# Loading the merge's numerators through GpSimd's queue and issuing its stores one step later, in a hybrid attention layer

## The chip, the cores and the metric

The kernel runs on 1 core of one Trainium2 chip. The metric is device time in microseconds (us) of the whole program; lower is better. A core has five engines that each take their instructions in order: TensorE (PE in the profile), VectorE (DVE), ScalarE (ACT), GpSimd (POOL) and SyncE (SP). A transfer (DMA) is issued by one of them, from its own place in that engine's order: an issue that has to wait holds up whatever stands behind it on the same engine. All queues share the core's 16 DMA engines.

## What is computed

One inference step of a decoder layer: 1,024 prompt rows and 64 sample rows (together 1,088) of width 2,048.

```
h = x @ w_in + b_in               # split into q, k, v, z_a | 3 x (q_g, k_g, v_g), z_b | g_a, g_b
o_a = sliding-window attention with sinks (16 heads)
o_b = sum_g softmax_g(lse_g) * dilated attention g    # g = 0..2, 8 heads each
y_a = o_a * silu(z_a);  y_b = o_b * silu(z_b)
m = sigmoid(g_a) * (y_a @ w_br_a) + sigmoid(g_b) * (y_b @ w_br_b)
x = LayerNorm(alpha * x + m @ w_out)
```

It also returns the new key and value windows.

## The kernel before

All products run on TensorE in three passes: every float32 operand is split into a high and a low part, and hi\*hi, lo\*hi and hi\*lo are added up in PSUM (lines 170 to 172). The input projection has 78 column tiles of 128. The first 34 (q, k, v) come first; while the other 44 (z, g_a, g_b) are multiplied, attention, decoding and last the **merge** are worked off beside them. Then follow the two output products, in three parts.

The order is written out by hand. `in_proj` calls `tick` once per 12 matmuls (4 rows of k by 3 products), here called a *step*; a column tile has 12 steps. `Beside.tick` first runs what was put off with `after(n, f)` for n steps, and then lets the background generator advance at a set rate, 0.9 of its own steps per step during the merge. Every engine therefore has one fixed order in which the projection's work and the merge's work alternate:

- **ACT**: casts a weight part to its high half (L89), evacuates a column tile from PSUM with the bias (L954), computes the merge's sigmoids (L865) and issues the merge's stores (L890).
- **DVE**: makes the low half of a weight part (L90), and does the merge's multiplications and additions (L854, L858, L859, L866, L867).
- **SP**: issues the weight loads (L78, 512 KB), the stores of the evacuated tiles (L956, 192 or 160 KB) and, before the change, the merge's loads of numerators (L841).
- **POOL**: issues the merge's loads of w (L844) and of z (L847).

Weight parts are split two parts ahead of the matmuls that use them (`Weights.ahead`, 4 buffers). A tile z of the projection has 2 buffers, so an evacuation L954 waits until the store L956 of the tile but one before has landed.

The merge goes over 12 rows of heads, i = 0..11. For i < 8 (mixer A) there is one *item*, (i, 0); for i = 8..11 (mixer B) there are three, (i, 0), (i, 1) and (i, 2). `load(i, g)` brings the numerator num(i, g) (544 KB for g = 0, 512 KB otherwise), the weights w(i, g) as two broadcasts of 256 KB each, and with g = 0 also z(i), 544 KB. `add(i, 0)` multiplies num by w (L854); `add(i, 1)` and `add(i, 2)` multiply (L858) and add to the numerator of g = 0 (L859). `gate(i, half)` computes o \* z \* sigmoid(z) in place of z (L865, L866, L867), and y(i), 544 KB, is stored from there.

Buffers decide what a load waits for: num with g > 0 has one buffer, so num(i, 2) waits for L858 of (i, 1), and num(i+1, 1) for L858 of (i, 2). w has two, so w(i, 2) needs the buffer that add(i, 0) has finished with. num with g = 0 has two, and waits for the gates of i-2. z has two, and z(i+2) waits until the store y(i) has landed.

Loads are called one item ahead (`steps`): at item n the next item's `load` stands before `add(n)`, but the load of (i, 2) stands after `add(i, 1)`.

Of the kernel before, what the change touches and what calls it, by code (L numbers as in the profile page):

```python
# [105 lines left out]
def layer_kernel(ctx: ExitStack, tc: tile.TileContext, A, O, S):  # L106
    nc = tc.nc
# [24 lines left out]
    def after(n, f):  # L132

        later.append((now[0] + n, f))
# [75 lines left out]
    with tc.tile_pool(name="qp", bufs=2, side="right") as qp:  # L210
# [152 lines left out]
        for g in range(4):  # L363
            w = (128,) + WINS
            n = w[g] - NQ
# [465 lines left out]
    def merge():  # L831
        with tc.tile_pool(name="mp", bufs=1, side="right", reuse_waits="tile") as mp:
            wb = weights_b(mp)
            items = [(i, g) for i in range(12) for g in range(1 if i < 8 else 3)]
            got, zs = {}, {}

            def load(i, g):
                num = mp.tile([P, T], F32, tag="num" if g else "o", name="num", bufs=1 if g else 2)
                w = mp.tile([P, NT], F32, tag="w", name="w", bufs=2)
                n = NT if g else T  # L840
                nc.sync.dma_start(out=num[:, :n], in_=S["num"][i + 4 * g, :, :n])  # L841
                src = S["wa"][2 * i:2 * i + 2] if i < 8 else S["wb"][g, 2 * (i - 8):2 * (i - 7)]
                for h in range(2):
                    nc.gpsimd.dma_start(out=w[HD * h:HD * (h + 1)], in_=src[h].partition_broadcast(HD))  # L844
                if g == 0:
                    zs[i] = mp.tile([P, T], F32, tag="z", name="z", bufs=2)
                    nc.gpsimd.dma_start(out=zs[i], in_=S["z"][i])  # L847
                got[i, g] = num, w

            def add(i, g):  # L850
                num, w = got[i, g]
                o = got[i, 0][0]
                if g == 0:
                    nc.vector.tensor_mul(o[:, :NT], o[:, :NT], w)  # L854
                    return
                nv = num[:, :NT].rearrange("p (c j) -> p j c", c=DILS[g])
                wv = w.rearrange("p (j c) -> p j c", c=DILS[g])
                nc.vector.tensor_mul(wv, nv, wv)  # L858
                nc.vector.tensor_add(o[:, :NT], o[:, :NT], w)  # L859

            def gate(i, half):
                c = slice(T // 2 * half, T // 2 * (half + 1))
                o, z = got[i, 0][0], zs[i]
                sg = mp.tile([P, T // 2], F32, tag="sg", name="sg")
                nc.scalar.activation(sg, z[:, c], AF.Sigmoid)  # L865
                nc.vector.tensor_mul(z[:, c], z[:, c], sg)  # L866
                nc.vector.tensor_mul(z[:, c], z[:, c], o[:, c])  # L867

            def steps():
                load(0, 0)  # L870
                for _ in range(3):
                    yield
                for n, (i, g) in enumerate(items):
                    nxt = items[n + 1] if n + 1 < len(items) else (0, 2)
                    if nxt == (8, 0):
                        for _ in wb:
                            pass
                    if nxt[1] < 2:
                        load(*nxt)
                    yield  # L880
                    add(i, g)
                    if g == 1:
                        load(*nxt)
                    yield
                    if nxt[0] != i:
                        gate(i, 0)
                        yield
                        gate(i, 1)
                        yield
                        nc.scalar.dma_start(out=S["y"][i], in_=zs[i])  # L890

            for _ in steps():
                next(wb, None)
                yield
# [107 lines left out]
    for part, (a, b) in enumerate(CHUNKS):  # L1002
        last = part == len(CHUNKS) - 1
        n = b - a
# [111 lines left out]
        if not last:  # L1116
            after(2, lambda: nc.scalar.activation(m4[:, :, 2], m4[:, :, 1], AF.Sqrt, bias=epst))
            nxt = load_g(0, *CHUNKS[part + 1])
            for i, (t, c) in enumerate(tiles):
                h, v = hs[i], mv[:, 4 * i:4 * i + 4]  # L1120
                after(3, lambda v=v: norm_start(v))
                for u in range(0, DM, 512):
                    n = 4 + 14 * i + 3 * (u // 512)
# [3 lines left out]
                        out=O["y"][t:t + P, u:u + 512], in_=h[:, u:u + 512]))  # L1127
# [130 lines left out]
```

## Time and profile before

| | us |
|---|---|
| median of 3 runs | 2760.76 (2759.12 to 2764.41) |
| the profiled execution, its own time | 2763.79 |
| its span | 2761.8 |
| PE busy | 2727.9 (99%) |
| DVE busy | 1477.8 (54%) |
| ACT busy | 928.5 (34%) |
| POOL busy | 855.2 (31%) |

The page's slices show PE at nine tenths or more in all but the first and the last, with a granted clock of 0.995 on average. The merge lies between 1883 and 2055 us of the span. In this stretch the DMA engines move 45.56 MB, 265 GB/s on average, where the whole span has 169 GB/s. The profile gives the time from issue to landing only for DMAs that POOL issues; for those of SP and ACT it is seen where somebody waits for the landing.

### The profile page before, as it was taken

What the parts mean: (1) busy time and instruction counts of PE and PEld (TensorE: products, weight loads), DVE (VectorE), ACT (ScalarE), POOL (GpSimd) and SP (SyncE); (2) the same over time, 40 slices, a digit from 0 to 9 for tenths busy, and PEclk for the clock granted to TensorE, in tenths of its full rate; (3) what the DMA queues carried; (4) which work ended last, traced back from release to release, by engine and by line L of the source; (5) the groups of instructions that cost most, each with busy time, mean ns of one, the idle gap of its engine ahead of it and who ended that gap; (6) DMA issues with size and microseconds to landing.
All of it is one profiled execution on the core that took longest, in us unless ns stands there. A gap on an engine that the chain in (4) does not pass through costs nothing.

```text
span 2761.8 us, 43516 instructions
## 1 busy us (share of the span) xinstructions
PE 2727.9 (99%) x16643; PEld 2625.8 (95%) x16643; DVE 1477.8 (54%) x2648; ACT 928.5 (34%) x1857; POOL 855.2 (31%) x905
## 2 busy tenths in 40 slices
PE   8999999999999999999999999999999999999997
PEld 8999999999999999999999998889999989988986
DVE  5444442443436777777665432124555556855866
ACT  4122222222223444444433332223224434433442
POOL 1112122131126666677677723433110000000001
PEclk9999999999999999999999999999999999999999
DMA  7345454464464333454445534657876745754763
GB/s 227 102 129 178 161 183 156 142 203 153 161 222 126 113 113 109 129 151 145 145 146 147 149 102 155 198 186 220 277 243 232 245 129 172 235 187 137 244 221 99
DMA packets 206088, 467.64 MB, mean 169 GB/s; under 512 B 28936, under 2 KB 128648, under 8 KB 203128
## 3 DMA queue, kind: packets, MB, share of 16 engines
q1 hardware_dynamic: 167512, 312.33, 35.8%
q0 software_dynamic: 36272, 145.19, 16.7%
q10 hardware_dynamic: 2096, 7.34, 0.7%
q8 instruction: 131, 2.15, 0.3%
q14 instruction: 77, 0.63, 0.1%
HBM read 365.17 MB, written 144.21 MB: 184 GB/s over the span
## 4 chain that ended last, share of the span: by engine, by line
PE 90%; DMA 4%; DVE 4%; ACT 1%; issue 1%; SPq 0%; POOL 0%; ACTq 0%; DVEq 0%; POOLq 0%
PE psd L170 21%; PE psd L172 21%; PE psd L171 21%; PE psd L1064 3%; PE psd L1063 3%; PE psd L1062 3%; PE psa L425 2%; PE psd L1021 2%; PE psd L1020 2%; PE psd L1019 2%; PE psa L487 1%; PE psa L486 1%; PE psa L1064 1%; PE psa L1063 1%; PE psa L1062 1%; PE psa L1021 1%
## 5 line engine op out<-in xcount | busy, mean ns | idle before, releaser
L170 PE MATMUL psd<-xhi,whi 128*128 128x384 f32 (+1 forms) x3712 | 1224.3, 330 | 16.8 <-ACT whi L89 12.3
L172 PE MATMUL psd<-xhi,wlo 128*128 128x384 f32 (+1 forms) x3712 | 1217.5, 328 | 0.5 <-DVE wlo L90 0.4
L171 PE MATMUL psd<-xlo,whi 128*128 128x384 f32 (+1 forms) x3712 | 1216.7, 328 | 0.1
L170 PEld LDWEIGHTS psd<-xhi,whi 128*128 128x128 f32 x3712 | 699.1, 188 | 32.9 <-issue 14.0
L90 DVE TENSOR_TENSOR wlo<-wraw,whi 128x512 fp32r<-128x512 f32 x648 | 449.0, 713 | 478.4 <-ACT whi L89 473.9
L172 PEld LDWEIGHTS psd<-xhi,wlo 128*128 128x128 f32 x3712 | 698.6, 188 | 2.0 <-DVE wlo L90 2.0
L171 PEld LDWEIGHTS psd<-xlo,whi 128*128 128x128 f32 x3712 | 699.1, 188 | 0.4 <-DVE xlo L226 0.4
L89 ACT CAST whi<-wraw 128x512 fp32r<-128x512 f32 x648 | 386.7, 618 | 393.2 <-PE psa L1063 151.7
L460 POOL PARTITION_ALL_REDUCE md<-s x160 | 310.1, 1938 | 67.2 <-ACT s L457 44.0
L446 POOL PARTITION_ALL_REDUCE md<-s x160 | 214.4, 1340 | 177.5 <-DVE s L435 65.0
L1126 POOL DMA_DIRECT2D o_y<-h x24 | 13.0, 542 | 573.0 <-DVE h L994 562.4
L477 DVE TENSOR_TENSOR pl<-s,ph 128x512 fp32r<-128x512 f32 (+1 forms) x160 | 128.0, 800 | 100.3 <-ACT ph L476 98.3
L1062 PE MATMUL psd<-whi,m 128*128 128x512 f32 x384 | 149.8, 390 | 0.5 <-ACT whi L89 0.5
L1063 PE MATMUL psd<-whi,m 128*128 128x512 f32 x384 | 149.8, 390 | 0.0
L1064 PE MATMUL psd<-wlo,m 128*128 128x512 f32 x384 | 149.7, 390 | 0.0
L457 ACT ACTIVATE s<-s 128x256 f32<-128x256 f32 (+1 forms) x160 | 75.9, 475 | 196.2 <-DVE s L456 196.0
L954 ACT ACTIVATE z<-psd,bias 128x384 f32<-128x384 f32 x132 | 73.8, 562 | 191.9 <-PE psd L172 126.2
L312 POOL DMA_DIRECT2D s_sq<-raw x20 | 11.5, 576 | 371.9 <-DVE raw L295 371.9
L1021 PE MATMUL psd<-y,wlo 128*128 128x384 f32 (+1 forms) x384 | 125.7, 327 | 0.1
L1019 PE MATMUL psd<-y,whi 128*128 128x384 f32 (+1 forms) x384 | 125.4, 326 | 0.0
L1020 PE MATMUL psd<-y,whi 128*128 128x384 f32 (+1 forms) x384 | 125.4, 326 | 0.0
L284 ACT ACTIVATE raw<-psd,bias 128x384 f32<-128x384 f32 (+1 forms) x79 | 44.2, 559 | 199.4 <-PE psd L172 199.4
(209 smaller groups left out, 3314.4 us busy)
## 6 DMA issues: line engine op xcount, KB each, us to landing
wraw<-w_in SPq DMA_DIRECT2D x152, 512.0 KB
wraw<-w_out SPq DMA_DIRECT2D x96, 512.0 KB
wraw<-w_br SPq DMA_DIRECT2D x72, 512.0 KB
o_c<-c POOLq DMA_DIRECT2D x64, 510.0 KB, 8.5
qst<-s_qs SPq DMA_DIRECT2D x80, 256.0 KB
s_zg<-z SPq DMA_DIRECT2D x64, 192.0 KB
kv<-ktb POOLq DMA_DIRECT2D x48, 256.0 KB, 3.7
kv<-vb POOLq DMA_DIRECT2D x48, 256.0 KB, 3.2
```

The source lines that it names most:

```text
L89: self.nc.scalar.copy(hi, raw)
L90: self.nc.vector.tensor_tensor(out=lo, in0=raw, in1=hi.bitcast(F32), op=ALU.subtract)
L170: nc.tensor.matmul(o, lhsT=h, rhs=xhi[k][:, a:b], start=(k == 0), stop=False)
L171: nc.tensor.matmul(o, lhsT=h, rhs=xlo[k][:, a:b], start=False, stop=False)
L172: nc.tensor.matmul(o, lhsT=l, rhs=xhi[k][:, a:b], start=False, stop=(k == KT - 1))
L446: nc.gpsimd.partition_all_reduce(u["md"][:, 0], top, P, RED.max)
L460: nc.gpsimd.partition_all_reduce(u["md"][:, 1], s[:, 1 if n == 1 else 2], P, RED.add)
L1019: nc.tensor.matmul(o, lhsT=h, rhs=yt[k][:, 0, :n], start=st, stop=False)
L1021: nc.tensor.matmul(o, lhsT=l, rhs=yt[k][:, 0, :n], start=False, stop=en)
L1062: nc.tensor.matmul(pt, lhsT=h, rhs=whi, start=st, stop=False)
L1063: nc.tensor.matmul(pt, lhsT=l, rhs=whi, start=False, stop=False)
L1064: nc.tensor.matmul(pt, lhsT=h, rhs=wlo, start=False, stop=en)
```

## The change

Two lines of `merge` are changed. The loads of numerators are issued by GpSimd instead of SyncE, at the head of each `load`; and the store of y(i) is put off by one step, so that it stands behind the next step's work in ACT's order.

```
@@ -838,7 +838,7 @@
                 n = NT if g else T
-                nc.sync.dma_start(out=num[:, :n], in_=S["num"][i + 4 * g, :, :n])
+                nc.gpsimd.dma_start(out=num[:, :n], in_=S["num"][i + 4 * g, :, :n])
@@ -887,7 +887,7 @@
                         gate(i, 1)
                         yield
-                        nc.scalar.dma_start(out=S["y"][i], in_=zs[i])
+                        after(1, lambda z=zs[i], i=i: nc.scalar.dma_start(out=S["y"][i], in_=z))
```

On POOL, at the end of the merge, where the rows i = 9 to 11 of mixer B are loaded, stood before:

```order
L844 DMA w<-s_wb 64x1024 x6
L847 DMA z<-s_z 128x1088
L844 DMA w<-s_wb 64x1024 x6
L847 DMA z<-s_z 128x1088
L844 DMA w<-s_wb 64x1024 x4
```

and now, from z(10) on:

```order
L847 DMA z<-s_z 128x1088
L841 DMA num<-s_num 128x1024
L844 DMA w<-s_wb 64x1024 x2
L841 DMA num<-s_num 128x1024
L844 DMA w<-s_wb 64x1024 x2
L841 DMA num<-s_num 128x1088
L844 DMA w<-s_wb 64x1024 x2
L847 DMA z<-s_z 128x1088
```

Every pair of loads of w now stands behind the load of its numerator, and so behind what that load waits for.

On SP, in the same part of the merge, a piece of the difference:

```order
-L841 DMA num<-s_num 128x1024
-L841 DMA num<-s_num 128x1088
-L78 DMA wraw<-w_in 128x1024
-L841 DMA num<-s_num 128x1024
-L78 DMA wraw<-w_in 128x1024
-L956 DMA s_zg<-z 128x384 x2
-L841 DMA num<-s_num 128x1024
+L78 DMA wraw<-w_in 128x1024 x2
+L956 DMA s_zg<-z 128x384 x2
+L956 DMA s_zg<-z 128x320
```

All 20 loads of numerators are gone from SP; the weight loads and the stores of evacuated tiles stand alone there.

On ACT, at one of the places where its order changes (a store of y, L890):

```order
 L865 ACTIVATE sg<-z 128x544
 L954 ACTIVATE z<-psd,bias 128x320
+L89 CAST whi<-wraw 128x512
 L890 DMA s_y<-z 128x1088
-L89 CAST whi<-wraw 128x512
```

The cast that stood behind the store now stands ahead of it. On PE and DVE nothing moves.

## Rows read from the trace of the kernel before

**Rows 1.** Waits of PE from 1883 to 2055 us: total, times, longest
```profile
PE psd L170 <- ACT whi L89: 5.2, 1, 5.2
PE psd L170 <- ACT z L954: 4.4, 2, 2.5
```

**Rows 2.** Windows of 20 us: length, busy per engine (instructions), PE's granted clock, DMA share, GB/s
```profile
1920.00:1940.00 20.00, 17.45 (x106) 17.13 (x105) 14.73 (x20) 6.20 (x10) 3.69 (x8) 1.00 0.79 259
...
1960.00:1980.00 20.00, 20.00 (x122) 20.00 (x121) 7.16 (x9) 5.87 (x10) 4.18 (x8) 1.00 0.91 299
1980.00:2000.00 20.00, 14.79 (x78) 13.98 (x77) 13.20 (x13) 2.21 (x4) 3.61 (x7) 0.83 0.81 242
```

**Rows 3.** ACT in order of time: start, length, what [idle before, what ended it]
```profile
1928.53 1.28 ACT L865 ACT_TABLE_LOAD   x1 [8.66 <-DMA z<-s_z]
...
1993.92 0.53 ACT L954 ACTIVATE z<-psd,bias 128x320 f32<-128x320 f32 x1 [15.51 <-DMA s_zg<-z]
```

**Rows 4.** SP in order of time; a row spans its issues and the waits between them
```profile
1964.35 18.73 SPq L841 DMA_DIRECT2D num<-s_num  x3
...
1983.65 11.14 SPq L956 DMA_DIRECT2D s_zg<-z  x3
...
2013.69 0.39 SPq L841 DMA_DIRECT2D num<-s_num  x1
```

**Rows 5.** DVE in order of time: L858 of the items with g > 0, and two low halves
```profile
1980.05 2.03 DVE L858 TENSOR_TENSOR w<-num,w 128x1024 f32<-128x1024 f32 x1 [6.51 <-DMA w<-s_wb]
...
1986.14 2.01 DVE L858 TENSOR_TENSOR w<-num,w 128x1024 f32<-128x1024 f32 x1 [2.20 <-DMA num<-s_num]
...
1994.98 0.69 DVE L90 TENSOR_TENSOR wlo<-wraw,whi 128x512 fp32r<-128x512 f32 x1 [4.18 <-ACT whi L89]
...
1999.05 2.03 DVE L858 TENSOR_TENSOR w<-num,w 128x1024 f32<-128x1024 f32 x1 [0.24 <-DMA num<-s_num]
...
2007.17 2.02 DVE L858 TENSOR_TENSOR w<-num,w 128x1024 f32<-128x1024 f32 x1 [3.31 <-DMA num<-s_num]
...
2021.98 2.03 DVE L858 TENSOR_TENSOR w<-num,w 128x1024 f32<-128x1024 f32 x1 [2.87 <-DMA num<-s_num]
...
2027.81 2.03 DVE L858 TENSOR_TENSOR w<-num,w 128x1024 f32<-128x1024 f32 x1 [1.93 <-DMA num<-s_num]
...
2040.09 2.03 DVE L858 TENSOR_TENSOR w<-num,w 128x1024 f32<-128x1024 f32 x1 [3.80 <-DMA w<-s_wb]
...
2046.19 2.02 DVE L858 TENSOR_TENSOR w<-num,w 128x1024 f32<-128x1024 f32 x1 [1.54 <-DMA num<-s_num]
...
2052.23 0.68 DVE L90 TENSOR_TENSOR wlo<-wraw,whi 128x512 fp32r<-128x512 f32 x1
```

**Rows 6.** PE in order of time, at the merge's end
```profile
2052.97 0.44 PE L172 MATMUL psd<-xhi,wlo 128*128 128x384 f32 x1
```

**Rows 7.** POOL in order of time: one load of z, three pairs of loads of w
```profile
1919.50 0.56 POOL L847 DMA_DIRECT2D z<-s_z  x1 [9.51 <-DMA s_y<-z]
...
1971.92 1.02 POOL L844 DMA_DIRECT2D w<-s_wb  x2 [1.34 <-DVE num L854]
...
1989.70 1.03 POOL L844 DMA_DIRECT2D w<-s_wb  x2 [4.51 <-DVE num L859]
...
2010.75 1.03 POOL L844 DMA_DIRECT2D w<-s_wb  x2 [6.55 <-DVE num L859]
```

**Rows 8.** Time to landing, line 844 (w, 256 KB) and then line 847 (z, 544 KB)
```profile
DMA to landing us min/median/max: 3.6/7.2/9.9
...
DMA to landing us min/median/max: 4.0/8.4/11.3
```

**Rows 9.** The chain that ended last: start, length, what
```profile
1994.88 4.05 DMA num<-s_num
```

**Rows 10.** A window of 2 us: length, PE busy (instructions), granted clock, DMA share, GB/s
```profile
1980.00:1982.00 2.00, 2.00 (x14) 1.00 0.02 8
```

**Rows 11.** Waits of ACT from 1883 to 2055 us: total, times, longest
```profile
ACT whi L89 <- DVE z L867: 10.3, 5, 2.5
```

More of the change, by code (lines that the diff above doesn't have):

```diff
@@ L840, in load @@
                 n = NT if g else T
-                nc.sync.dma_start(out=num[:, :n], in_=S["num"][i + 4 * g, :, :n])
+                nc.gpsimd.dma_start(out=num[:, :n], in_=S["num"][i + 4 * g, :, :n])
                 src = S["wa"][2 * i:2 * i + 2] if i < 8 else S["wb"][g, 2 * (i - 8):2 * (i - 7)]
@@ L889, in steps @@
                         yield
-                        nc.scalar.dma_start(out=S["y"][i], in_=zs[i])
+                        after(1, lambda z=zs[i], i=i: nc.scalar.dma_start(out=S["y"][i], in_=z))
             for _ in steps():
```

## The prediction

> **What bounds the kernel now.** I looked first at what PE waits for, stretch by stretch. In the merge's stretch it waits three times, 5.2 us for a cast and twice, 4.4 us in all, for an evacuation [rows 1]; the change touches no other stage, so I set no term elsewhere. Counting matmuls gives the same loss with the clock in it: an undisturbed 20 us hold 122, so one takes 0.164 us, while 1920 to 1940 us hold 106 and 1980 to 2000 us only 78 [rows 2]. That is 16 x 0.164 = 2.6 us and 44 x 0.164 = 7.2 us; the second has 5.2 us of standing and 2.0 us of the clock, which after PE had stood was granted at 0.83 on average, part of the window at 1.2 instead of 2.4 GHz. The third wait is 4.4 - 2.5 = 1.9 us. Together **11.7 us, 0.42% of the time, is all that the change can win**.
>
> Then I asked what stood behind these waits. For the first, ACT sat 8.66 us until z(3) had landed [rows 3], and z(3) had been issued only after 9.51 us of waiting for the store y(1) to land [rows 7]: a loop of store, landing, load, landing over two items. For the second, ACT sat 15.51 us until an earlier tile's store had landed [rows 3]. SP issued that store at 1983.65, because its three loads of numerators from 1964.35 on filled 18.73 us [rows 4]: num(8, 2) had to wait for L858 of (8, 1), which ran from 1980.05 to 1982.08 [rows 5]. While SP stood there the DMA engines were nearly empty, share 0.02 from 1980 to 1982 us [rows 10].
>
> At the merge's end another limit shows. The last low half that DVE makes inside the merge ends at 2052.23 + 0.68 = 2052.91 [rows 5], and PE's first product with it starts at 2052.97 [rows 6]. DVE is just in time: no reserve is left. What DVE's chain of merge items gains or loses up to there, PE gains or loses one for one, within the 11.7 us. So I add up that chain.
>
> **The change part by part.**
>
> *SP loses 20 issues.* Short in themselves, and PE never waits for SP's issuing. What counts is where they waited. Num(9, 1) could have gone at 1986.14 + 2.01 = 1988.15 [rows 5] and went at 1994.88 [rows 9], 6.7 us late, behind a tile's store that itself waited for ACT. Num(10, 1) could have gone at 2009.19 [rows 5] and went at 2013.69 [rows 4], 4.5 us late. Both held L858. Without them w is the next to come late: w(9, 1), second half issued at 1990.2 [rows 7], lands by the median of 7.2 us [rows 8] at 1997.4, and L858 began at 1999.05 [rows 5]: 1.65 us won. For w(10, 1) it is 2011.26 + 7.2 = 2018.5 against 2021.98: 3.5 us. At (11, 1) the wait was for w already [rows 5], nothing won. **Sum -5.2 us**, bounds 0 (w still later) and -11.2 (w beside num).
>
> *DMA time that lay idle is filled.* The weight load and the two stores behind num(8, 2), 512 + 2 x 192 KB, start before 1980 us instead of after 1983. At 299 GB/s [rows 2] they are 3.1 us of traffic taken out of the crowd after it. I take the 2.0 us of rows 10: **-2.0 us**, bounds 0 and -3.1.
>
> *POOL gains 20 issues of half a microsecond* [rows 7], as much as one issue of w; POOL is busy 3 to 4 of 20 us [rows 2], so that is covered by its waiting. Were that cover gone, 20 x 0.51 = 10 us would stand on the path. The cost is in the order. Before, w(8, 2) was issued at 1971.92 [rows 7], 8 us ahead of L858 of (8, 1). Now it stands behind num(8, 2), which waits for that L858, and so in each of the four rows of mixer B. The numerator alone took 4.05 us from issue to use [rows 9]; now the next L858 needs the numerator and 512 KB behind it. Added: 0.2 us for the slower issue (0.51 against some 0.3) and 512 KB at 299 GB/s, 1.75 us, so 1.95 us each. **4 x 1.95 = +7.8 us.** No row shows this directly. From below, w's data hide in the numerator's and only the 1.0 us of issuing and the 0.2 remain: +4.8. From above, w takes its median 7.2 us [rows 8] from its second issue, 1.0 us after the numerator's: 8.2 - 4.05 = 4.15 each, +16.6. I take 1.95, nearer to the lower end, since w then follows a queue that has just run empty and the shortest landing is 3.6 us [rows 8].
>
> *The order between z and num.* Num(i+1, 0) now stands behind z(i), which waits for a store to land. It is needed only after the gates of i, by which time z(i) has landed and been used, so this costs nothing; if it landed late, add(i+1, 0) would wait, about 2 us each time. But z(i) no longer has that numerator ahead of it in the DMA engines, 544 KB or 1.86 us at 299 GB/s.
>
> *The store one step later.* One step is 12 x 0.164 = 1.97 us. ACT's casts no longer wait for DVE's gate: 10.3 us in five waits [rows 11], which I count as nothing by themselves, since ACT is busy 6 of 20 us [rows 2] and PE met only the three waits above. The loop of y and z gets longer by up to 1.97 us; on the other hand y(i+1) too now falls behind z(i+2), another 1.86 us off z. Each loop: -2 x 1.86 + 1.97 = -1.75 us. Three such loops in a row lead up to L858 of (8, 1); I count two, since the merge's own pace, 0.9 of its steps per step, takes the rest. **-3.5 us**, bounds 0 and -5.3.
>
> Sum: -5.2 - 2.0 + 7.8 - 3.5 = **-2.9 us**. The profiled execution took 2763.79 us, 2.0 more than its span, and would take 2760.9; it lies 3.0 us above the median, so for the median 2760.76 - 2.9 = **2757.9 us**. A measurement of this kernel can tell about 0.2%, 5.5 us, from no change, so this is a forecast of no visible change, on the fast side.
>
> **The rivals.**
>
> *Most of the loss comes back.* The second PE wait came from SP's blocking alone: DVE too sat 4.18 us for that cast [rows 5]. If w costs only the lower bound (+4.8) and the loops and the idle time give their upper ones (-5.3, -3.1, with -5.2 as above), the chain is 8.8 us shorter: 2752.0 us. For it speaks that the traffic needs less than the time: 299 GB/s were reached where 242 were moved in the worst window [rows 2]. Against it, that DVE has no reserve at the end [rows 6].
>
> *Slower: the loss of the early w.* The four distances from L858 of (i, 1) to that of (i, 2) are 6.1, 8.1, 5.8 and 6.1 us [rows 5], mean 6.5. If w lands at its median behind the numerator, each grows by 4.15 us, and if nothing of the idle DMA time is won, 16.6 - 8.7 = +7.9 us: 2768.7 us. The point from which the change loses is 10.7/4 = 2.7 us more per pair, a distance of 9.2 us; it is visible from some 4 us more, 10.5 us. For it speaks that w's landing was 7.2 us in the median [rows 8]; against it, that much of that was queueing behind loads which now go elsewhere.
>
> *GpSimd's transfers start later than SyncE's.* Loads of 256 KB from POOL landed at best after 3.6 us [rows 8]; the 512 KB from SP took 4.05 [rows 9], and 3.2 without 256 KB at 299 GB/s: up to 0.4 us later per load. Two per row of mixer B stand on the chain, 8 x 0.4 = 3.4 us with the fraction kept, and the time is 2761.3. Against it stands a 544 KB load of POOL that landed after 4.0 us [rows 8]. The Trainium skill, "DMA: Bandwidth & Descriptors", Specifications, gives a first byte after about 1 us on GpSimd's path and 0.6 us on SyncE's, and its section "Issuing engine by pattern" puts simple loads on SyncE: by that rule the move is wrong, and an estimate from that page's figures is 8 x 0.4 = 3.2 us. On this rule the trace does not decide: its two rows point to either side.
>
> **How the numbers follow.** My forecast gets 0.38, the later start 0.10, the recovery 0.34, the loss of the early w 0.18. The first two are within 0.2%: 0.48; faster 0.34, slower 0.18. The forecast's own range, with the later start in it, is the band within 0.2%, 2755.3 to 2766.3. The range for 8 in 10 goes down to 2750.5, near the 2749.1 at which PE waits for nothing in the merge, and up to 2767.0, short of the slow rival's full price.
>
> **What would show it.** In the changed profile SP's stores should follow their evacuations at once, and the wait of 15.51 us for such a store should be gone. L858 of (8, 1) should begin earlier than 1980.05; the distances within a pair should grow from 6.5 to some 8.5 us, and those from (i, 2) to (i+1, 1) shrink from 12.9, 14.8 and 12.3. PE should lose 8 to 9 us instead of 11.7, most of it late in the merge and for DVE's low halves or casts behind L858. I am wrong if distances within a pair stay at 6.5 us (then faster), if they pass 10.5 us (then slower), or if PE waits outside the merge change.

## The result, and the profile after

The changed kernel is **slower**: 2779.56 us in the median (2773.18 to 2784.8, 4 runs) beside 2761.36 (4 runs) of the kernel before, a ratio of 1.0065 with an interval of 1.005 to 1.0079. The loss is 18.2 us, and the time lies outside the forecast's range. The profiled execution took 2784.8 us, the longest of the four, and is 21.0 us longer than the profiled one of before (2763.79), so what the traces show of the loss is somewhat more than the medians do.

PE's waits come first, as before, now with the waits of the two engines that this change concerns. Waits of the kernel after, from 1883 to 2100 us: engine and line waiting, what it waited for, total, times, longest.

```profile
POOL num L841 <- DVE w L858: 61.4, 7, 13.4
...
DVE w L858 <- DMA w<-s_wb: 43.1, 7, 8.7
...
ACT z L954 <- DMA s_zg<-z: 25.0, 6, 5.7
...
PE psd L170 <- ACT z L954: 10.0, 3, 6.2
...
PE psd L172 <- DVE wlo L90: 8.8, 3, 4.7
...
PE psd L170 <- ACT whi L89: 3.0, 1, 3.0
```

PE stands for 10.0 + 8.8 + 3.0 = 21.8 us where it stood for 9.6 [rows 1], and 8.8 of them are for DVE's low halves, for which it had not waited at all. The store that held ACT for 15.51 us [rows 3] holds it for 5.7 at most now: that wait is gone, and the time did not come with it. Two lines have come to the top. POOL waits 61.4 us in seven places to issue a numerator, because the numerator's one buffer is free only once L858 has run; and DVE's L858 in turn waits 43.1 us in seven places for w, where it had waited for w 10.3 us in two.

Windows of the kernel after, columns as in [rows 2]; the last three are short ones inside the others.

```profile
1920.00:1940.00 20.00, 17.77 (x97) 17.46 (x96) 17.73 (x26) 9.99 (x15) 5.29 (x10) 0.91 0.92 254
1940.00:1960.00 20.00, 18.44 (x113) 18.12 (x112) 9.07 (x13) 4.44 (x9) 4.76 (x9) 1.00 0.99 313
1980.00:2000.00 20.00, 13.10 (x71) 12.46 (x69) 8.02 (x7) 2.16 (x4) 5.07 (x10) 0.87 0.66 183
2000.00:2020.00 20.00, 15.88 (x82) 15.56 (x82) 10.39 (x11) 1.99 (x4) 4.24 (x9) 0.84 0.80 228
2020.00:2040.00 20.00, 17.00 (x86) 17.00 (x87) 10.76 (x12) 4.22 (x8) 4.96 (x10) 0.77 0.89 277
2060.00:2080.00 20.00, 15.99 (x86) 15.41 (x85) 9.21 (x11) 5.02 (x9) 0.00 (x0) 0.91 0.30 94
1981.00:1987.00 6.00, 4.61 (x29) 4.29 (x27) 2.15 (x2) 1.05 (x3) 0.00 (x0) 1.00 0.17 59
1998.00:2006.00 8.00, 5.09 (x18) 5.09 (x19) 6.01 (x8) 2.46 (x4) 1.49 (x3) 0.57 1.02 263
2009.00:2011.00 2.00, 2.00 (x13) 2.00 (x12) 1.97 (x2) 0.00 (x0) 0.19 (x1) 1.00 0.05 18
```

Against 122 matmuls in an undisturbed 20 us, the six windows lack 25 + 9 + 51 + 40 + 36 + 36 = 197, by 0.164 us each 32.3 us. Before it was 11.7. The difference, 20.6 us, is the 21.0 us by which the profiled executions differ: nearly the whole loss lies in the merge, most of it after 1980 us, in mixer B. Some of it is the clock's: after PE stood, 0.77 to 0.91 were granted on average where full windows have 1.00. And the DMA engines still run empty in between, at a share of 0.17 from 1981 to 1987 us and of 0.05 from 2009 to 2011.

DVE of the kernel after in order of time, the rows that answer to [rows 5], L858 of the items with g > 0:

```profile
1984.82 1.95 DVE L858 TENSOR_TENSOR w<-num,w 128x1024 f32<-128x1024 f32 x1 [8.34 <-DMA w<-s_wb]
...
1995.69 1.91 DVE L858 TENSOR_TENSOR w<-num,w 128x1024 f32<-128x1024 f32 x1 [7.06 <-DMA w<-s_wb]
...
2008.48 2.03 DVE L858 TENSOR_TENSOR w<-num,w 128x1024 f32<-128x1024 f32 x1 [3.94 <-DMA w<-s_wb]
...
2017.48 1.89 DVE L858 TENSOR_TENSOR w<-num,w 128x1024 f32<-128x1024 f32 x1 [5.11 <-DMA w<-s_wb]
...
2028.54 2.02 DVE L858 TENSOR_TENSOR w<-num,w 128x1024 f32<-128x1024 f32 x1
...
2038.84 2.02 DVE L858 TENSOR_TENSOR w<-num,w 128x1024 f32<-128x1024 f32 x1 [6.42 <-DMA w<-s_wb]
...
2050.81 2.03 DVE L858 TENSOR_TENSOR w<-num,w 128x1024 f32<-128x1024 f32 x1 [3.49 <-DMA w<-s_wb]
...
2063.39 2.02 DVE L858 TENSOR_TENSOR w<-num,w 128x1024 f32<-128x1024 f32 x1 [8.69 <-DMA w<-s_wb]
```

The distances from (i, 1) to (i, 2) are 10.9, 9.0, 10.3 and 12.6 us, mean 10.7, where they were 6.5. Those from (i, 2) to (i+1, 1), called *gaps* below, are 12.8, 11.1 and 12.0 where they were 12.9, 14.8 and 12.3. L858 of (8, 1) comes 4.8 us later than before, and all waits that end here now end with w.

Why w is late is seen on POOL, kernel after, in order of time:

```profile
1987.06 0.56 POOL L841 DMA_DIRECT2D num<-s_num  x1 [13.37 <-DVE w L858]
1987.61 1.05 POOL L844 DMA_DIRECT2D w<-s_wb  x2
1988.62 0.56 POOL L841 DMA_DIRECT2D num<-s_num  x1
1989.17 1.05 POOL L844 DMA_DIRECT2D w<-s_wb  x2
1990.18 0.57 POOL L847 DMA_DIRECT2D z<-s_z  x1
1997.90 0.54 POOL L841 DMA_DIRECT2D num<-s_num  x1 [7.14 <-DVE w L858]
...
2053.14 0.56 POOL L841 DMA_DIRECT2D num<-s_num  x1 [9.66 <-DVE w L858]
```

POOL stands 13.37 us for L858 of (8, 1). Behind it stand not only w(8, 2) but num(9, 0), w(9, 0) and z(9), and within 3.7 us they all go out: 2.6 MB with num(8, 2), on one queue. They land in the order of issue: num(8, 2) at 1991.3, the second half of w(8, 2) at 1995.5, num(9, 0) at 1999.5, z(9) at 2004.9. The next numerator, num(9, 1), is issued at 1997.90 behind the rest of them. The chain that ended last shows how long these transfers took. Kernel after: start, length, what.

```profile
1972.12 10.81 DMA num<-s_num
...
1987.06 4.25 DMA num<-s_num
...
1997.90 8.60 DMA num<-s_num
...
2010.81 4.11 DMA num<-s_num
...
2019.67 4.65 DMA num<-s_num
...
2030.85 4.03 DMA num<-s_num
...
2041.16 8.04 DMA num<-s_num
...
2054.19 9.08 DMA w<-s_wb
```

There are two kinds. Num(8, 2), num(9, 2) and num(10, 2) (1987.06, 2010.81, 2030.85), issued when the loads ahead of them on POOL's queue had landed, take 4.0 to 4.3 us. Num(9, 1) and num(11, 1) (1997.90, 2041.16), issued behind the burst, take 8.6 and 8.0, where num(9, 1) took 4.05 on SP's queue [rows 9]; num(10, 1) between them got through in 4.65. These last three came in right behind what was still ahead of them: 1.6, 1.7 and 1.3 us after z(9), z(10) and z(11), which took 14.7, 8.7 and 13.9 us. From issue to landing, z(9) to z(11), kernel after:

```profile
DMA to landing us min/median/max: 8.7/13.9/14.7
```

Num(8, 1), issued right behind z(8), takes 10.81. One row does not fit: num(11, 2), issued at 2053.14 with all loads ahead of it landed and only its own w behind it, took 9.1 us, and why stays open.

### The profile page after: what moved, and what is told of

Read it like the earlier page. It is cut to its first block, busy times and chain, and to the rows that moved or that the text cites. A ratio compares the mean times of both kernels' runs of the same rounds, so it can differ in the third digit from the quotient of the medians.

```text
span 2783.0 us, 43507 instructions
## 1 busy us (share of the span) xinstructions
PE 2731.8 (98%) x16643; PEld 2628.0 (94%) x16643; DVE 1476.7 (53%) x2648; ACT 928.2 (33%) x1857; POOL 866.2 (31%) x925
## 4 chain that ended last, share of the span: by engine, by line
PE 87%; DMA 6%; DVE 3%; issue 2%; ACT 1%; POOL 0%; SPq 0%; ACTq 0%; POOLq 0%; DVEq 0%
PE psd L170 20%; PE psd L172 20%; PE psd L171 20%; PE psd L1062 3%; PE psd L1064 3%; PE psd L1063 3%; PE psa L425 2%; PE psd L1020 2%; PE psd L1019 2%; PE psd L1021 2%; DMA num<-s_num 2%; PE psa L487 1%; PE psa L486 1%; PE psa L1062 1%; PE psa L1064 1%
## 5 line engine op out<-in xcount | busy, mean ns | idle before, releaser
L312 POOL DMA_DIRECT2D s_sq<-raw x20 | 11.5, 576 | 372.2 <-DVE raw L295 372.2
```

## The experiments

Five theories were put to the test. **1**: w comes late because it stands behind its own numerator. **2**: the later store delays y and z. **3**: a numerator that goes through GpSimd's queue is slower in itself. **4**: the numerator's wait for its one buffer, harmless in SP's order, is what costs once it stands in POOL's. **5**: too much is on one queue, so the transfer that is needed next comes in behind others that are not. Each of the kernels e1 to e12 was timed in five rounds, 5 to 12 executions. The table has the median of the kernel and of the kernel before on the same chip, the recorded ratio with its interval, and from the one profiled execution the distances within pairs and the gaps, worked out from the starts of L858. The ratio is not the quotient of the two medians, which differs by up to 0.1% (by the medians e3 would be 1.0050, e4 and e6 1.0009, e5 1.0042); losses of 0.1 or 0.2% are therefore uncertain.

| kernel | median us | before | ratio, interval | within pairs | gaps |
|---|---|---|---|---|---|
| before | | | | 6.1 8.1 5.8 6.1 | 12.9 14.8 12.3 |
| after | 2779.56 | 2761.36 | 1.0065, 1.005 to 1.0079 | 10.9 9.0 10.3 12.6 | 12.8 11.1 12.0 |
| e1 loads alone | 2776.20 | 2762.25 | 1.0056, 1.0043 to 1.0068 | 9.2 9.0 9.9 11.3 | 10.8 12.0 10.2 |
| e2 store alone | 2761.44 | 2762.25 | 0.9997, 0.9989 to 1.0006 | 5.8 8.5 5.7 6.8 | 14.2 13.1 13.4 |
| e3 w first | 2776.14 | 2762.25 | 1.0043, 1.0027 to 1.0058 | 6.1 6.1 6.9 7.7 | 16.5 13.3 16.7 |
| e4 only g = 0 moved | 2764.21 | 2761.69 | 1.0014, 1.0005 to 1.0023 | 6.3 7.4 7.9 6.1 | 12.5 11.4 12.4 |
| e5 only g > 0 moved | 2773.27 | 2761.69 | 1.005, 1.0038 to 1.0063 | 11.8 11.9 11.5 12.1 | 8.7 10.8 9.0 |
| e6 changed, two buffers | 2764.29 | 2761.69 | 1.0017, 1.0008 to 1.0026 | 3.7 7.4 3.8 4.0 | 11.7 12.7 15.9 |
| e7 before, two buffers | 2760.74 | 2761.69 | 1.0003, 0.9993 to 1.0012 | 3.8 4.7 3.8 3.9 | 13.6 13.8 15.2 |
| e8 short queue | 2767.61 | 2761.71 | 1.0019, 1.0008 to 1.003 | 6.3 7.5 6.7 8.7 | 9.9 13.8 11.3 |
| e9 only g > 0, two buffers | 2761.86 | 2761.71 | 1.0, 0.999 to 1.001 | 3.7 8.9 3.8 3.8 | 11.7 12.7 15.4 |
| e10 rate 0.8 | 2753.58 | 2761.71 | 0.9965, 0.9951 to 0.9978 | 6.9 5.9 6.7 6.5 | 12.4 14.7 16.7 |
| e11 rate 0.8, two buffers | 2750.43 | 2761.71 | 0.9957, 0.9944 to 0.9971 | 3.8 5.5 3.8 3.8 | 13.2 14.7 16.6 |
| e12 changed, rate 0.8 | 2761.68 | 2762.17 | 0.9998, 0.9989 to 1.0007 | 10.2 14.4 10.1 9.3 | 11.1 10.2 11.0 |

### The two edits one by one: e1 and e2

e1 has the change's first line alone, e2 its second.

```
e1:
-                nc.sync.dma_start(out=num[:, :n], in_=S["num"][i + 4 * g, :, :n])
+                nc.gpsimd.dma_start(out=num[:, :n], in_=S["num"][i + 4 * g, :, :n])
e2:
-                        nc.scalar.dma_start(out=S["y"][i], in_=zs[i])
+                        after(1, lambda z=zs[i], i=i: nc.scalar.dma_start(out=S["y"][i], in_=z))
```

> The loads of numerators on GpSimd as in the changed kernel, but each store of y at once as before. Theory 1 (w now stands behind its numerator, which waits for L858; four pairs of mixer B grow from 6.5 to 10 us or more): still slow, 2772 to 2782 us, and the four distances within a pair stay at 9 to 12.5 us. Theory 2 (the later store lengthens the loop of y and z): nearly all of the loss gone, 2756 to 2766 us. Theory 3 (transfers that GpSimd issues are slower in themselves): slow as under theory 1.

> The loads of numerators stay on SyncE, only the store of y comes one step later. Theories 1 and 3: no visible change, 2756 to 2766 us, distances within a pair 6 to 8 us. Theory 2: slow, 2770 us or more.

The loads alone cost 0.56%, the store alone nothing that can be told. Theory 2 falls. Whether the store adds a little on top of the loads (1.0065 against 1.0056) stays open, since the intervals overlap.

### w ahead of its numerator: e3

Against the changed kernel, within `load`:

```
-                nc.gpsimd.dma_start(out=num[:, :n], in_=S["num"][i + 4 * g, :, :n])
                 src = S["wa"][2 * i:2 * i + 2] if i < 8 else S["wb"][g, 2 * (i - 8):2 * (i - 7)]
                 for h in range(2):
                     nc.gpsimd.dma_start(out=w[HD * h:HD * (h + 1)], in_=src[h].partition_broadcast(HD))
+                nc.gpsimd.dma_start(out=num[:, :n], in_=S["num"][i + 4 * g, :, :n])
```

> Both edits, but within a load the two halves of w are issued ahead of the numerator, all from GpSimd. Theory 1: w(i, 2) goes out early again, the distances within a pair fall back to 6 to 8.5 us, and the time to 2752 to 2766 us. Theory 2 and theory 3: the same loads come from the same queue and the store is as late, so it stays at 2772 us or more.

The distances within pairs were back at 6.1 to 7.7 us, as theory 1 has it, and the time was not: still 0.43% above. What the pairs won the gaps lost, 13.3 to 16.7 us. The chain that ended last of e3 names the transfer:

```profile
1983.50 3.76 DMA num<-s_num
...
1991.95 11.84 DMA num<-s_num
...
2006.25 3.67 DMA num<-s_num
...
2014.56 6.62 DMA num<-s_num
...
2025.70 4.51 DMA num<-s_num
...
2034.85 12.02 DMA num<-s_num
```

The second, fourth and sixth are num(i+1, 1), issued 6 to 7 us after num(i+1, 0), with w and z(i+1) between: 6.62 to 12.02 us to the landing where num(i, 2) took 3.67 to 4.51. So w's place behind its numerator is one form of the delay, and with w moved ahead the delay falls on num(i+1, 1) instead; theory 1 alone does not explain the loss. The same rows speak against theory 3: a numerator through GpSimd's queue can land after 3.7 us, no later than the 4.05 seen on SP's.

### Which numerators: e4 and e5

Against the changed kernel:

```
e4:
-                nc.gpsimd.dma_start(out=num[:, :n], in_=S["num"][i + 4 * g, :, :n])
+                (nc.sync if g else nc.gpsimd).dma_start(out=num[:, :n], in_=S["num"][i + 4 * g, :, :n])
e5:
-                nc.gpsimd.dma_start(out=num[:, :n], in_=S["num"][i + 4 * g, :, :n])
+                (nc.gpsimd if g else nc.sync).dma_start(out=num[:, :n], in_=S["num"][i + 4 * g, :, :n])
```

> Both edits, but only the 12 numerators with g = 0 go through GpSimd; the 8 with g = 1 and 2 stay on SyncE. Theory 4 (a numerator with g > 0 waits for L858, and on GpSimd's queue that wait holds all loads of the merge behind it, which then go out in one burst, ahead of what the next L858 needs): the loss is gone, 2756 to 2768 us, distances within a pair 6 to 8.5 us, L858 on average 20 us from item row to item row. Theory 3 (GpSimd's transfers are slower in themselves): 12 of 20 loads are slower, 2768 to 2776 us.

> Both edits, but only the 8 numerators with g = 1 and 2 go through GpSimd; those with g = 0 stay on SyncE. Theory 4: nearly all of the loss stays, 2770 to 2782 us, distances within a pair 9 us or more. Theory 3: 8 of 20 loads are slower, 2765 to 2770 us.

The twelve g = 0 numerators, for whose buffers POOL waits 7.9 us in e4, cost 0.14%, just clear of nothing (1.0005 to 1.0023); the eight with g > 0, for whose buffer it waits 60.4 us in e5, cost 0.50%. Together that is, within the intervals, the change's 0.65%. In e5 num(9, 1), num(10, 1) and num(11, 1) land 3.5 to 4.5 us after their issue, so little holds them up on the way; instead its pairs are long, 11.5 to 12.1 us. There it is w that L858 waits for (42.3 us in seven places): w(i, 2) goes out only behind num(i, 2), and that only after L858 of (i, 1).

### Two buffers: e6, e7 and e9

The numerators with g > 0 get a second buffer; to make room, a small tile of the merge moves into one of an earlier stage. e6 is the changed kernel with it, e7 the kernel before, e9 the changed kernel with it and with g = 0 back on SP.

```
-        top = mp.tile([32, 256], F32, tag="top", name="top", bufs=1)
+        top = masks[:32, 0:2].rearrange("p a b -> p (a b)")
...
-                num = mp.tile([P, T], F32, tag="num" if g else "o", name="num", bufs=1 if g else 2)
+                num = mp.tile([P, T], F32, tag="num" if g else "o", name="num", bufs=2)
e9 also:
+                (nc.gpsimd if g else nc.sync).dma_start(out=num[:, :n], in_=S["num"][i + 4 * g, :, :n])
```

> The changed kernel with two buffers for the numerators with g > 0 (the room comes from the masks, no longer read by then), so that num(i, 2) no longer waits for L858 of (i, 1). Theory 4: the distances within a pair fall to 3 to 7 us and the time to 2750 to 2766 us. Theory 3: the same transfers from the same queue, 2772 us or more.

> The kernel before with the same two buffers, so that SyncE is not held by a numerator that waits for L858 just before it. If SyncE's blocking was what cost PE its second wait (as the prediction has it): PE loses 3 to 8 us in the merge instead of 11.7, and the time is 2752 to 2758 us. If DVE's chain is bound by the DMA engines' rate alone: no visible change, 2757 to 2766 us.

> Two buffers for the numerators with g>0; only these on GpSimd's queue, g=0 on SyncE's, the merged tile stored one step later. Theory 4 (the loss is the wait for the buffer, which now stands in GpSimd's in-order queue; the rest comes from the g=0 numerators): with neither, the time is that of the kernel before, 2757 to 2766 us. If the move of the numerators costs something apart from this wait, 2768 us or more.

e6 falls from 0.65% to 0.17%, and e9, with the g = 0 numerators back on SP, to nothing (1.0, 0.999 to 1.001). e9 differs from e5 by the second buffer alone: eight numerators through GpSimd's queue cost 0.50% with one buffer and nothing that can be told with two, and e7 shows that the buffer by itself changes nothing. Theory 4 holds for the main part, and theory 3 falls for these eight. What the twelve g = 0 numerators cost (0.14% in e4, 0.17% in e6) has no cause shown: their longer issue on POOL, their place behind z or the fuller queue are all possible. In e6 POOL's waits for L858 are gone from the list of waits.

e7 is the surprise. In it SP stands for L858 only 3.6 us in two places (19.3 in five before), and DVE's chain is well ahead of before. The last L858, (11, 2), of e7 and then of e6:

```profile
2036.35 2.01 DVE L858 TENSOR_TENSOR w<-num,w 128x1024 f32<-128x1024 f32 x1
...
2040.91 2.02 DVE L858 TENSOR_TENSOR w<-num,w 128x1024 f32<-128x1024 f32 x1
```

In e7 it starts at 2036.35 instead of 2046.19 [rows 5], 9.8 us earlier, in an execution of 2757.02 us. That execution is the shortest of e7's eleven, and PE waits 6.0 us in its merge beside 9.6, so it flatters the kernel; over all runs the ratio is 1.0003. In e6 the chain ends 5.3 us earlier than before, in an execution of 2764.33 us, 0.5 us longer than the one of before. A gain in DVE's chain as large as the prediction's first one could be had, and was worth nothing that can be told.

### A short queue: e8

Against e3, the g = 0 numerators and mixer B's z go through SP, so that little is ahead of num(i+1, 1) on GpSimd's queue.

```
-                nc.gpsimd.dma_start(out=num[:, :n], in_=S["num"][i + 4 * g, :, :n])
+                (nc.gpsimd if g else nc.sync).dma_start(out=num[:, :n], in_=S["num"][i + 4 * g, :, :n])
...
-                    nc.gpsimd.dma_start(out=zs[i], in_=S["z"][i])
+                    (nc.gpsimd if i < 8 else nc.sync).dma_start(out=zs[i], in_=S["z"][i])
```

> The numerators with g>0 stay on GpSimd's queue (the pair's w issued ahead of them, the merged tile stored one step later), but the g=0 numerators and mixer B's loads of z go through SyncE's queue, so that the next item's first numerator stands behind little on GpSimd's queue. Theory 5 (the one in-order queue carries too much: the urgent numerator waits behind w, z and another numerator): the next item's first numerator lands 4 to 8 us after its issue instead of 10 to 12, the gaps between pairs shrink from 13-17 to 13 us or less, 2758 to 2766 us. Theory 3 (a numerator through GpSimd's queue is slower in itself): landings stay near 10 us, 2770 us or more.

The chain that ended last of e8, num(9, 1), num(10, 1) and num(11, 1):

```profile
1990.54 5.21 DMA num<-s_num
...
2007.89 7.06 DMA num<-s_num
...
2028.46 6.57 DMA num<-s_num
```

They land after 5.2 to 7.1 us instead of 6.6 to 12.0, the gaps shrink to 9.9, 13.8 and 11.3, and the loss halves from 0.43% to 0.19%. That agrees with theory 5 as far as landings go; the time, 2767.61, is 1.6 us above what it gave. Two limits belong to this: the profiled execution took 2761.5 us, the shortest of twelve, so its distances may flatter the kernel, and e4 has shown that the g = 0 numerators alone are worth 0.14%, so how much of the 0.24% is the shorter queue of z stays open.

### The pace: e10, e11 and e12

One number is changed, in the kernel before (e10), in e7 (e11) and in the changed kernel (e12):

```
-RATES = (1.0, 1.15, 0.9)
+RATES = (1.0, 1.15, 0.8)
```

> The kernel before with the merge's rate 0.8 instead of 0.9 generator steps per step, so that the merge spreads over more steps. If what PE loses in the merge comes from work asked for faster than DMA and VectorE deliver it, PE loses less: 2750 to 2757 us. If the loss lies elsewhere, 2758 to 2766 us.

> The kernel before with rate 0.8 and two buffers for the numerators with g>0. If the merge is asked for too fast, 2749 to 2757 us, no slower than rate 0.8 alone; the second buffer alone was worth nothing, so if the rate is worth nothing too, 2758 to 2766 us.

> The changed kernel as it is, with the merge's rate 0.8 instead of 0.9. At 0.8 an undisturbed item is asked for every 20.3 us (from the kernel with rate 0.8 and two buffers: starts of the first multiplication at 2001.89, 2022.11, 2042.51), at 0.9 thus every 18.0; the changed kernel's items came every 22.0 us on average. If the change costs what its loop is longer than the pace asked, its cost falls with the pace: 18.0 of 4 us an item before, some 1.7 us an item now, 2757 to 2768 us, still above the 2753.6 of rate 0.8 alone. If the change's cost does not depend on the pace, it stays at 0.65% above rate 0.8 alone: 2769 to 2774 us.

The slower pace makes the kernel before faster by 0.35%. In the merge of e11 PE waits only 1.6 us, in one place, between 1940 and 1960 us. Windows of e11 after that:

```profile
1980.00:2000.00 20.00, 20.00 (x124) 20.00 (x123) 12.22 (x12) 3.62 (x6) 3.26 (x7) 1.00 1.02 293
...
2020.00:2040.00 20.00, 20.00 (x123) 20.00 (x122) 12.83 (x13) 5.17 (x9) 3.61 (x7) 1.00 0.94 307
```

The windows are full, at full clock, with the DMA engines busy throughout. Both e10 and e11 beat the kernel before and the changed one; whether the second buffer adds anything (0.9957 against 0.9965) the intervals don't tell. The change costs 0.33% at this pace (0.9998 against 0.9965), where it costs 0.65% at the old one: its cost depends on the pace. In e12's profile the distances are as long as in the changed kernel, 9.3 to 14.4 us, but PE's waits in the merge's stretch are 6.5 us in two places, all for low halves, instead of 21.8. The contrast is somewhat overdrawn, since e12's profiled execution is the shortest of its eleven and the changed kernel's the longest of its four.

## Why the prediction was wrong

**What was right.** The stage and the order of events: SP's stores follow their evacuations, the 15.51 us wait is gone, distances within pairs grow, PE is late for low halves behind L858. The slower rival stood in the right place too: w behind a numerator that waits for L858. Its sign for "visibly slower", a mean distance of 10.5 us, was passed at 10.7. The limit of 11.7 us on any gain was not tested by the change; the largest gain here, e11's, is 11.3 us.

The sum of the prediction can be put beside what DVE's chain did in the two profiles. L858 of (8, 1) starts 4.8 us later, where -3.5 was booked. The four pairs grow by 16.6 us in all, where +7.8 was booked. The three gaps shrink by 4.2 us, where SP's blocking was to give -5.2 and -2.0. So the last L858 starts 17.2 us later, and so does the product that waits for the last low half. Kernel after, DVE and PE at the merge's end:

```profile
2069.44 0.69 DVE wlo L90
...
2070.17 0.69 PE psd L172
```

The low half ends at 2070.13, against 2052.91 before, and PE starts with it at once. Of the remaining 3.8 of the 21.0 us part is the clock's (0.91 on average from 2060 to 2080 us); the rest is not accounted for.

**The step that failed first: what w costs.** The prediction took +1.95 us each, "since w then follows a queue that has just run empty". From the issue of num(i, 2) to the next L858 it would then have been 4.05 + 1.95 = 6.0 us, and 8.2 by its upper bound. It was 1995.69 - 1987.06 = 8.6, 2017.48 - 2010.81 = 6.7, 2038.84 - 2030.85 = 8.0 and 2063.39 - 2053.14 = 10.3, mean 8.4. The pairs grew by 10.7 - 6.5 = 4.2 us, the upper bound of 4.15: 4 x 4.2 = +16.8 instead of +7.8. The queue was empty only in front of the numerator. In the first three rows the next item's load is released at the same moment, which the reason given did not consider; that it is what makes w late is not shown, since the fourth row, with no such load behind it, is the longest. In e1 and e5, slow too with w behind its numerator, the pairs are likewise 9.0 to 12.1 us.

**The second: gains of DVE's chain are not PE's one for one.** "No reserve is left", read from one low half at the end, was true for losses, as the rows above show. For gains it was wrong: e6's chain is 5.3 us ahead with no gain in time, and e7, with SP's wait for L858 nearly gone, shows 1.0003, by its interval a gain of 1.9 us at most. So the -5.2 and the -2.0 that go with SP's blocking would hardly have shown as a faster kernel; in the changed one the shorter gaps took 4.2 us off what the chain lost elsewhere. The slower rival set 8.7 us of such gains against its 16.6. Without this offset it gives 2760.76 + 16.6 = 2777.4 us, 2.2 below what was measured. That this comes so near is partly luck: in the profile the gaps' 4.2 us and the late start's 4.8 nearly cancel.

**The third: z, num(i, 0) and the store.** -3.5 was booked, and L858 of (8, 1) was to come earlier than 1980.05. It came at 1984.82. Num(8, 1) took 10.81 us behind z(8). This delay is not common to the slow kernels: in e1 that L858 starts at 1979.66, in e5 at 1977.29. The later store alone gave nothing in time (e2), though that L858 started at 1977.08 in e2's profile; and the order of z and num, which "costs nothing", has at most a part in the 0.14% that e4 shows with the store in it.

**What neither forecast nor rival named** is that w's lateness is one form of a wait that holds everything behind it. Before, two in-order issuers each stood for its own buffers, and what one could not yet issue did not hold up the other's loads. After, POOL stands for both, and then issues all that had piled up at once: w(i, 2), needed first, goes out no earlier than its numerator, and num(i+1, 1), needed after it, comes behind the whole burst. Ordering within a load only moves the delay from the one to the other (e3); a buffer that removes the wait removes it (e9).

The rule of the Trainium skill that the prediction weighed ("DMA: Bandwidth & Descriptors", "Issuing engine by pattern": simple loads on SyncE) pointed the right way. The reason put beside it, the later first byte, is not what these runs show: e9 has eight numerators on GpSimd at no cost that can be told. The same page's section "🔬 Queues, rings and completion order" says that each DMA engine takes turns, packet by packet, between the queues that have work for it. By that a numerator on SP's queue would get a share at once beside what POOL's queue still has, and one on POOL's would wait its turn there. The trace agrees. Before, between 1994 and 1999.2 us, while num(9, 1) took its 4.05 us, both queues moved (packets, MB, share of 16 engines; q0 is POOL's, q1 SP's, q10 ACT's):

```profile
q1 hardware_dynamic: 357, 0.95, 62.0%
q0 software_dynamic: 112, 0.33, 26.2%
```

After, between 1998 and 2006 us, while num(9, 1) took 8.60:

```profile
q0 software_dynamic: 468, 1.64, 83.5%
q10 hardware_dynamic: 105, 0.42, 14.5%
q1 hardware_dynamic: 7, 0.03, 2.7%
```

The engines are at least as busy, at 263 GB/s where it was 249, but with what stood ahead of it: z(9), issued 7.7 us before num(9, 1), landed at 2004.9, 1.6 us before it. That the rule holds for every load is not shown by these windows.

## What to carry to other kernels

Before a load is moved to another engine, write down what it waits for and everything that stands behind it there: a load that waits for its only buffer belongs where nothing urgent follows, or needs a second buffer first. When such a wait ends, price the whole burst that it releases and ask whether the next urgent transfer is first or last in it; at about the same traffic num(9, 1) landed after 4 us when SP issued it, and after 8.6 on POOL's queue behind such a burst. And before any of this, try the pace of the background work: one number here was worth 0.35%, most of the 0.42% that the prediction had named as all there was to win.

## What the runs showed of the hardware that was not expected

A 512 KB numerator took between 3.67 and 12.02 us on the same queue in the same kernel (e3). POOL's queue carried 17.61 MB in the merge before (1883 to 2055 us) and 28.45 after (1883 to 2072); at 1.6 times the bytes the median landing of mixer B's w rose only from 7.1 to 8.1 us. So the bytes in all hardly tell how late a transfer comes: in the changed kernel z(9) took 14.7 us within a burst and num(10, 2) 4.0 in front of one. And a chain that ended 5.3 us earlier (e6) gave no time back, while the same work asked for more slowly did (e10).
